# A second projection pass in another order of its products, and x pairs in the value blocks' places

## The chip, the cores and the metric

The kernel runs on one core of a Trainium2 chip. The metric is the device time of one execution in microseconds (us). The kernel before takes 901.85 us, the median of three runs (900.83 to 902.15).

## What is computed

One decoder layer over 512 tokens of width 2048, in float32: a norm, one input projection, two groups of eight attention heads, gates, an output projection, a norm and the residual. `w_in` holds side by side the latents of the MLA heads (768 of the queries, 512 of the keys and values), a rotary key of 64, the MLA gate (1024), queries, keys and values of the FoX heads (1024 each), eight forget logits and the FoX gate (1024).

```python
h = _rms_norm(x, g_pre)
proj = h @ w_in
(q_lat, kv_lat, k_rope_raw, gate_mla,
 fq, fk, fv, f_logit, gate_fox) = jnp.split(proj, split_points, axis=-1)
o_mla = _mla_branch(q_lat, kv_lat, k_rope_raw, g_q, w_uq, g_kv, w_ukv, cos, sin) * jax.nn.silu(gate_mla)
o_fox = _fox_branch(fq, fk, fv, f_logit, b_forget) * jax.nn.silu(gate_fox)
o = jnp.concatenate([o_mla, o_fox], axis=-1) @ w_out
return x + _rms_norm(o, g_post)
```

In the MLA branch both latents are normed, and the queries are `q_lat @ w_uq`, the keys and values `kv_lat @ w_ukv`. In the FoX branch the scores get the running sums of the log forget gates added.

## The kernel before

**Numbers.** TensorE (PE) multiplies halves of a float32 number: each operand is divided into a rounded part `hi` and a rest `lo`, and a product is three matmuls, `hi*hi`, `hi*lo` and `lo*hi`, which stand on lines 152, 153 and 154. Weights come in chunks of 512 KB. `load` or `fill` (lines 236 to 243) brings a chunk into a buffer `raw` by DMA; `divide` (line 283) then makes `whi` on ScalarE (ACT, line 290) and `wlo` on VectorE (DVE, line 291).

**Seven products.** Two large projections are computed with seven block products in place of eight (a Strassen scheme): products `p1`, `p2`, `g5`, `g3`, `g7`, `q6`, `p4`, in which the weights are blocks B11, B12, B21, B22 or sums of them, and the x operand is a block of `h` or a difference of blocks. Sums of weights are made by the DMA itself: a chunk is loaded by SyncE's queue (SP, line 241), and a second block is added into the same buffer by a DMA of GpSimd's (POOL, line 243). A chain, `follow`, says which later chunk takes over a buffer: once a chunk is divided, `fill` of the next one is issued into the same buffer. In the order of before, `g5` begins the chain with B12 in the first pass, and with B11 and an added B12 in the second; `g3` loads B22 afresh, and `g7`, `q6` and `p4` each add one block to what is there.

**Passes.** The first pass, "vg", makes the FoX values (v) and the FoX gate (g), about 65 to 200 us; its `p1` and `p2` accumulate in banks `va` and `ga`. Then come the FoX heads, to about 440 us. The second pass, "lm", makes the MLA latents (l) and the MLA gate (m), with banks `la`, `ma`, then `lg`, `mg`, `lc`, `mc`, `lp`, `mp`, up to 590 us. The MLA heads follow (`mq` and `mk` are queries and keys of a pair of heads, `uA` and so on their values, `sm` scores), and the output projection from about 750 us.

**x operands.** `x_steps(j)` (line 1108) makes, for each of four groups j of the contraction, a pair `xr` of float32 x blocks from `hi` and `lo` (line 1116), and hands it to `away_steps` (line 996), whose `make` computes the four differences `rmg` (line 1015), divides the first into `smg`, and sends each two of them to DRAM (`awaymg`, by POOL, line 1005). `fetch` (line 1044) brings them back as `bmg` or `bmq` when a product needs them, and `part_fetched` divides them (lines 141 and 142, on ACT and DVE). The pairs and the differences lie in the common places `slot` (28 of them).

**Order.** Each engine works through its own queue in order. Which instruction stands where is set by a scheduler from the order of the code; steps put into `todo` are drawn between matmuls, and lists given to `one(..., side=...)` go between the chunks of one product. The forget gate's steps are `forget_sums`, `fs[:3]` and `fs[3:]`: among the latter the transposes `rf` (line 839), its copy (line 840) and the running sum `fz` (line 846). `fox_q` (line 1125) gives the first queries, `fq`, scaled to `fqr` on DVE (line 1130).

**Latents.** `latent(i)` squares a latent block and adds it up in `ls`; `stats_steps` turn a sum (`lbk` of the keys, `lbq` of the queries, by matmuls on PE, line 1471) into a factor, `latent_row(1)` spreads the keys' factor over the partitions (`lrk`, by matmuls), and `latent_part(i)` makes the divided operands `ln`. `mla_k` and the values use `ln6` to `ln9`, the queries `ln0` to `ln5`; `raw153` to `raw155` are the first three chunks of `w_uq`.

Of the kernel before, what the change touches and what calls it, by code (L numbers as in the profile page):

```python
# [19 lines left out]
P = 128  # L20
# [45 lines left out]
def tile_hybrid_layer(  # L66
# [350 lines left out]
    B11, B12, B21, B22 = ((h, c) for h in range(2) for c in range(2))  # L417
    REST = ("g3", B22, None), ("g7", None, B12), ("q6", None, B11), ("p4", None, B21)

    def add_fox(p, n):  # L420
# [6 lines left out]
    for g in "vg":  # L427
        up_chunks.update(prods["p2", g])
    for step in (("g5", None, B12), *REST):
        add_chain("vg", *step)  # L430
# [7 lines left out]
    for j in range(1, 4):  # L438
        chain["m", j] = prods["p2", "m"][j]
    for step in (("g5", B11, B12), *REST):  # L440
        add_chain("lm", *step)
    mla = [{} for _ in range(4)]
    for n in ("q0", "p1", "k0", "q6", "p2", "p4", "g7", "q1", "g5", "k1", "g3", "q2", "k2", "q3", "k3"):
        if (n, "u") in SEVEN:
            add_products([(n, "u")], plain_up)
            if n not in ("p1", "p4"):
                up_chunks.update(prods[n, "u"])
            continue
        p = int(n[1])
        if n[0] == "q":  # L450
            mla[p]["q"] = [
                i
                for k in (4, 0, 2)
                for i in add_chunks(
                    w_uq,
                    [
                        (0, 2 * QK * p, NOPE),
                        (NOPE, 2 * QK * p + QK, NOPE),
                        (2 * NOPE, 2 * QK * p + NOPE, ROPE),
                        (2 * NOPE + ROPE, 2 * QK * p + QK + NOPE, ROPE),  # L460
                    ],
                    2, 2, 2 * QK, k,
                )
            ]
            if p == 0:
                up_chunks.update(mla[p]["q"])
        else:
            mla[p]["k"] = add_chunks(
                w_ukv, [(0, 512 * p, NOPE), (NOPE, 512 * p + NOPE + DV, NOPE)], KVR // P, 4, 2 * NOPE
            )  # L470
# [637 lines left out]
    def x_steps(j):  # L1108

        pair = []  # L1110

        def whole(h, i):
            if not pair:
                pair.extend(slot(f"xr{n}{j}") for n in range(2))
            k = 2 * j + 8 * h + i
            dve.tensor_tensor(out=pair[h][:, i, :], in0=hh[k].bitcast(F32), in1=hl[k].bitcast(F32), op=ALU.add)
            if h and i:
                todo.extendleft(reversed(away_steps("m", j, pair, keep="g5")))

        return [lambda h=h, i=i: whole(h, i) for h in range(2) for i in range(2)]  # L1120
# [149 lines left out]
    wait(1)  # L1270
    todo.extend([*fs[3:], *x_steps(0), *x_steps(1)])
    places = [(g, j) for g in "vg" for j in range(4)]
# [54 lines left out]

    def products(gs, between, out=lambda g, c, half: None):

        G, C, B = {}, {}, {}  # L1330
        for name in ("g5", "g3", "g7", "q6", "p4"):
            for g in gs:
                bank_of = G if name in ("g5", "g3") else B if name == "p4" else C
                if name in ("g5", "p4"):
                    bank_of[g] = banks(name, g, g == gs[1])
                elif name == "g7":
                    C[g] = two_of(proj_bank, f"{g}c")
                rate, side = between.get((name, g), (1, ()))
                one(name, g, bank_of[g], name in ("g5", "g7", "p4"), rate, side)
                if name == "g5":  # L1340
                    place(g, 1, 1)
                    put(g, 1, 1, G[g], ALU.subtract, P1)
                elif name == "g3":
                    place(g, 1, 0)
                    put(g, 1, 0, G[g], ALU.subtract, P1)
                elif name == "g7":
                    put(g, 1, 0, C[g], "less")
                elif name == "q6":
                    put(g, 1, 0, C[g], ALU.add)
                    out(g, 1, 0)  # L1350
                    put(g, 1, 1, C[g], ALU.add)
                    out(g, 1, 1)
                    put(g, 0, 1, C[g], "less")
                else:
                    put(g, 0, 1, B[g], ALU.add)
                    out(g, 0, 1)
                between.get((name, g, "after"), lambda: None)()
# [11 lines left out]
    for g in "vg":  # L1369
# [4 lines left out]
    products(  # L1374
        "vg",
        {
# [58 lines left out]

    LAT = (("q", (4, 5, 0, 1, 2, 3), QR), ("k", (8, 9, 6, 7), KVR))
    raws_of = [None] * 5
# [3 lines left out]
    def raw(i):  # L1441
        return raws_of[(i // 2 + 1) % 5][:, i % 2, :]
# [77 lines left out]
    drain()  # L1520
    for i in (*prods["g5", "l"], prods["g5", "m"][0]):
        fill(i, slot(f"rawl{i}", shape=(P, 1024)))
# [10 lines left out]
    beside.append(room.enter_context(tc.tile_pool(name="rw", bufs=8, reuse_waits="tile")))  # L1533
    for f in f5:
        f()
# [3 lines left out]
    for i in range(2):  # L1539
        for t in range(NT):  # L1540
            pe.transpose(lb[i][:, t * P : (t + 1) * P], l4[:, t, i * P : (i + 1) * P], ident)
        latent(8 + i, lb[i])
    one("p2", "m", A["m"], False, side=[lambda: None, *d5[:2], lambda: (d5[2](), d5[3]())])
    place("m", 0, 0)
# [8 lines left out]

    def later_latents():
        todo.extend(lambda i=i: latent(i, raw(i)) for i in range(4, 8))
        todo.extend([*s1, lambda: latent_part(4), lambda: latent_part(5)])

    def first_latents():
        todo.extend(lambda i=i: latent_part(i) for i in range(4))
        todo.append(lambda: latent_row(1))  # L1560
        todo.extend(lambda i=i: latent_part(i) for i in range(6, 10))

    products(
        "lm",
        {
            ("g5", "l"): (1, f3), ("g5", "m"): (1, d3), ("g3", "l"): (1, f7), ("g3", "m"): (1, d7),
            ("g7", "l"): (1, f6), ("g7", "m"): (1, d6), ("q6", "m", "after"): later_latents,
            ("p4", "l", "after"): first_latents, ("p4", "m"): (2, ()),
        },
# [5 lines left out]
    room.close()  # L1575
    todo.extend(lambda i=i: latent(i, raw(i)) for i in range(4))
    todo.append(lambda: latent_stats(0))
# [7 lines left out]
    qnh, qnl = zip(*(latents[i] for i in LAT[0][1]))  # L1585
    knh, knl = zip(*(latents[i] for i in range(6, 10)))

# [5 lines left out]
    def halves(a):  # L1593
        return [a[:, t, :] for t in range(2)]

    todo.extend(operand_steps("u", 0, (raws_of[4], raws_of[0]), ("sums",), tmp, part_slot))

    def latent_x(half, tokens):
        def parts(kk, t):
            ts = slice((tokens + t) * P, (tokens + t + 1) * P)  # L1600
            return knh[2 * half + kk][:, ts], knl[2 * half + kk][:, ts]

        return parts
# [29 lines left out]
    def mla_k(p, wholes):  # L1633

        kb = [proj_bank(f"mk{p}{i}") for i in range(2)]
        proj_T(mla[p]["k"], [(kb[i], P, two[i]) for i in range(2)], knh, knl, 2, 6)
        kw = [[whole_block(wholes, 2 + i, kb[i]), krw] for i in range(2)]
# [284 lines left out]
```

## Time and profile before

| | |
|---|---|
| median of three runs | 901.85 us |
| the profiled execution's own time | 899.95 us |
| its span | 898.2 us |
| granted clock of TensorE, mean | 0.994 |
| POOL's DMA queue, share of 16 engines | 34.7% |
| SP's DMA queue, share of 16 engines | 48.1% |
| the DMA busy over the whole span, mean | 221 GB/s |

The page gives busy times of each engine, the span in 40 slices, the DMA queues, the chain of work that ended last, and groups of instructions by line. The trace behind it gives the same for any stretch, the waits of an engine with what ended them, and timelines. A busy time above 95% says that an engine leaves little to gain but its waits. The granted clock is the share of full speed at which TensorE ran. A DMA share of 1 says that all 16 engines are busy. Rows with "x3" hold three equal instructions.

### The profile page before, as it was taken

To read this page: it belongs to the slowest core of one execution; us is meant where nothing else is said; L and a number is where in the kernel's file an instruction comes from. 1 tells how busy PE (TensorE), PEld (TensorE's weight loads), DVE (VectorE), ACT (ScalarE), POOL (GpSimd) and SP (SyncE) were. 2 spreads that over 40 slices of the span, in tenths; PEclk is the share of its full clock that TensorE was granted. 3 is DMA by queue.
4 is the path that set the end of the run, shared out by engine and by line. 5 is a ranking of instruction groups with operands and counts; after the bars stand their busy time and mean duration, and the time that the engine had idled before them with its cause. 6 is when DMAs were issued, how large, how long until landed. Compare 5 with 4: busy or idle time off the path is not lost.

```text
span 898.2 us, 13763 instructions
## 1 busy us (share of the span) xinstructions
PE 877.7 (98%) x5078; PEld 773.3 (86%) x5078; DVE 624.6 (70%) x1055; ACT 499.1 (56%) x914; POOL 125.2 (14%) x132
## 2 busy tenths in 40 slices
PE   9999899999999999999989999999999999999996
PEld 8978799999888888889989999987888888887885
DVE  4597756667364744647556767899787886998786
ACT  6934454435245453545634545557676887646383
POOL 1023104451110100000211444000000000000021
PEclk9999999999999999999999999999999999999999
DMA  9499979998588788884799999566959546799878
GB/s 294 128 288 283 277 213 193 222 235 224 110 204 227 192 226 203 230 231 115 253 281 330 280 225 206 116 203 148 222 133 251 149 141 196 230 321 320 263 223 250
DMA packets 128488, 198.41 MB, mean 221 GB/s; under 512 B 16338, under 2 KB 61292, under 8 KB 127396
## 3 DMA queue, kind: packets, MB, share of 16 engines
q1 hardware_dynamic: 101428, 136.28, 48.1%
q0 software_dynamic: 26256, 61.02, 34.7%
q8 instruction: 40, 0.66, 0.3%
q10 hardware_dynamic: 736, 0.22, 0.1%
q14 instruction: 28, 0.23, 0.1%
HBM read 182.60 MB, written 44.25 MB: 253 GB/s over the span
## 4 chain that ended last, share of the span: by engine, by line
PE 79%; DMA 9%; DVE 6%; ACT 3%; issue 2%; POOL 1%; SPq 0%; DVEq 0%; POOLq 0%; ACTq 0%
DMA raw<-in_w_in_dram 5%; PE fk L152 3%; PE fk L154 3%; PE fk L153 3%; PE in L654 3%; PE fq L152 3%; PE fq L153 3%; PE sm L697 3%; PE fq L154 3%; DVE wlo L291 2%; PE mq L152 2%; PE mq L153 2%; PE mq L154 2%; PE sf L697 2%; PE oa L154 2%
## 5 line engine op out<-in xcount | busy, mean ns | idle before, releaser
L291 DVE TENSOR_TENSOR wlo<-raw,whi 128x1024 fp32r<-128x1024 f32 (+3 forms) x159 | 186.9, 1177 | 114.4 <-ACT whi L290 110.9
L290 ACT CAST whi<-raw 128x1024 fp32r<-128x1024 f32 (+3 forms) x159 | 160.5, 1011 | 151.6 <-PE fk L153 35.4
L152 PE MATMUL fk<-h,whi 128*128 128x512 f32 x128 | 52.5, 410 | 0.0
L152 PE MATMUL fq<-h,whi 128*128 128x512 f32 x128 | 50.9, 398 | 0.0
L154 PE MATMUL fk<-h,wlo 128*128 128x512 f32 x128 | 50.3, 393 | 0.0
L154 PE MATMUL fq<-h,wlo 128*128 128x512 f32 x128 | 50.1, 392 | 0.0
L153 PE MATMUL fk<-h,whi 128*128 128x512 f32 x128 | 50.1, 391 | 0.0
L153 PE MATMUL fq<-h,whi 128*128 128x512 f32 x128 | 50.0, 390 | 0.0
L290 ACT CAST whi<-rawv 128x1024 fp32r<-128x1024 f32 x24 | 25.2, 1049 | 42.9 <-PE gg L153 11.0
L291 DVE TENSOR_TENSOR wlo<-rawv,whi 128x1024 fp32r<-128x1024 f32 x24 | 29.3, 1225 | 22.9 <-ACT whi L290 21.3
L290 ACT CAST whi<-rawl 128x1024 fp32r<-128x1024 f32 x25 | 26.2, 1047 | 29.7 <-PE mc L153 7.6
L291 DVE TENSOR_TENSOR wlo<-rawl,whi 128x1024 fp32r<-128x1024 f32 x25 | 30.4, 1224 | 16.8 <-ACT whi L290 16.8
L290 ACT CAST whi<-rawg 128x1024 fp32r<-128x1024 f32 x24 | 25.2, 1052 | 29.6 <-PE vc L154 8.5
L291 DVE TENSOR_TENSOR wlo<-rawg,whi 128x1024 fp32r<-128x1024 f32 x24 | 29.3, 1224 | 13.5 <-ACT whi L290 13.5
L715 ACT ACTIVATE pf<-pf,stf 128x128 f32<-128x128 f32 (+3 forms) x32 | 18.0, 562 | 30.7 <-DVE stf L706 30.7
L243 POOL DMA_DIRECT2D rawl<-in_w_in_dram x20 | 23.9, 1198 | 52.5 <-PE ptf L724 30.9
L1742 POOL DMA_DIRECT2D c<-in_x_dram x8 | 7.0, 1011 | 171.4 <-ACT c L1741 171.4
L654 PE MATMUL in<-whi,h 128*128 128x328 f32 x128 | 30.0, 322 | 0.1
L152 PE MATMUL mq<-ln,whi 128*128 128x512 f32 x72 | 29.1, 404 | 0.0
L154 PEld LDWEIGHTS fk<-h,wlo 128*128 128x128 f32 x128 | 24.0, 188 | 5.3
L154 PEld LDWEIGHTS fq<-h,wlo 128*128 128x128 f32 x128 | 24.0, 188 | 5.3
L154 PE MATMUL mq<-ln,wlo 128*128 128x512 f32 x72 | 28.4, 394 | 0.0
(625 smaller groups left out, 2926.7 us busy)
## 6 DMA issues: line engine op xcount, KB each, us to landing
raw<-in_w_in_dram SPq DMA_DIRECT2D x62, 512.0 KB
raw<-in_w_out_dram SPq DMA_DIRECT2D x32, 512.0 KB
rawl<-in_w_in_dram POOLq DMA_DIRECT2D x20, 512.0 KB, 13.1
rawv<-in_w_in_dram POOLq DMA_DIRECT2D x16, 512.0 KB, 8.3
rawg<-in_w_in_dram POOLq DMA_DIRECT2D x16, 512.0 KB, 11.7
raw<-in_w_in_dram POOLq DMA_DIRECT2D x12, 512.0 KB, 11.2
bmg<-awaymg SPq DMA_DIRECT2D x20, 256.0 KB
rawl<-in_w_in_dram SPq DMA_DIRECT2D x10, 512.0 KB
```

The source lines that it names most:

```text
L152: pe.matmul(o, ah, bh, start=first, stop=False, **kw)
L153: pe.matmul(o, ah, bl, start=False, stop=False, **kw)
L154: pe.matmul(o, al, bh, start=False, stop=last, **kw)
L243: pool.dma_start(to, second, accum_op=ALU.add)
L290: act.copy(hi[:, :m], raw[:, :m])
L291: dve.tensor_tensor(out=lo[:, :m], in0=raw[:, :m], in1=hi[:, :m].bitcast(F32), op=ALU.subtract)
L654: pe.matmul(banks[t][:, :n], a[k][:, tss[t]], b[:, j, :], start=k == 0 and m == 0, stop=k == NK - 1 and m == 2,)
L697: pe.matmul(s[:, :nn], a[:, qs], c[:, :nn], start=(i == 0), stop=(i == len(pairs) - 1))
L715: act.activation(p, p, AF.Exp, bias=st[:, 0:1], scale=unit, accum_out=st[:, 1:2])
L1742: pool.dma_start(to, x[piece(t, c)], accum_op=ALU.add)
```

## The change

There are two parts.

The first concerns the x pairs. They are taken from `v_block`, the four blocks in the pool of the value tiles, and no longer from `slot`; and `x_steps(0)` goes into `todo` ahead of `fs[3:]`.

The second is the order in the second pass: `g3`, `g7`, `q6`, `p4`, `g5` for `g5`, `g3`, `g7`, `q6`, `p4`. `g3`'s chunks begin a chain with one load of B22, and `g5`'s end it with a load of B11 and an added B12. `products` is written so that both orders can be had: which result goes into which block of the output, and which banks are fresh, follow from the order. The operands of `g3` are the first to be fetched, those of `g5` are fetched and divided beside `q6`. With that, the latents come out in another order: 0 to 3 after `p4`, 4 to 9 after `g5`; the query latents are taken as 0 to 5 and `w_uq`'s chunks in the order 0, 2, 4; `latent_row(1)`, `latent_part(6)` to `(9)` and `latent(4)`, `latent(5)` stand behind the pass.

```diff
     REST = ("g3", B22, None), ("g7", None, B12), ("q6", None, B11), ("p4", None, B21)
+    FIRST, LAST_ONE = ("g5", None, B12), ("g5", B11, B12)
...
         chain["m", j] = prods["p2", "m"][j]
-    for step in (("g5", B11, B12), *REST):
+    for step in (*REST, LAST_ONE):
         add_chain("lm", *step)
...
                 i
-                for k in (4, 0, 2)
+                for k in (0, 2, 4)
                 for i in add_chunks(
...
             if not pair:
-                pair.extend(slot(f"xr{n}{j}") for n in range(2))
+                pair.extend(v_block(f"xr{n}{j}") for n in range(2))
             k = 2 * j + 8 * h + i
...
     wait(1)
-    todo.extend([*fs[3:], *x_steps(0), *x_steps(1)])
+    todo.extend([*x_steps(0), *fs[3:], *x_steps(1)])
     places = [(g, j) for g in "vg" for j in range(4)]
...
-    def products(gs, between, out=lambda g, c, half: None):
-
-        G, C, B = {}, {}, {}
-        for name in ("g5", "g3", "g7", "q6", "p4"):
+    def products(gs, names, between, out=lambda g, c, half: None):
+
+        o = {}
+        early = names[0] == "g5"
+        for name in names:
             for g in gs:
-                bank_of = G if name in ("g5", "g3") else B if name == "p4" else C
-                if name in ("g5", "p4"):
-                    bank_of[g] = banks(name, g, g == gs[1])
+                key = {"g3": "g5" if early else "g3", "q6": "g7"}.get(name, name), g
+                fresh = key not in o
+                if fresh:
+                    o[key] = two_of(proj_bank, f"{g}c") if name == "g7" else banks(name, g, g == gs[1])
+                a = o[key]
+                rate, side = between.get((name, g), (1, ()))
+                one(name, g, a, fresh, rate, side)
+                if name == "g3":
+                    place(g, 1, 0)
+                    put(g, 1, 0, a, ALU.subtract, P1)
                 elif name == "g7":
-                    C[g] = two_of(proj_bank, f"{g}c")
-                rate, side = between.get((name, g), (1, ()))
-                one(name, g, bank_of[g], name in ("g5", "g7", "p4"), rate, side)
-                if name == "g5":
+                    put(g, 1, 0, a, "less")
+                elif name == "p4":
+                    put(g, 0, 1, a, ALU.add)
+                    out(g, 0, 1)
+                elif name == "q6":
+                    put(g, 1, 0, a, ALU.add)
+                    out(g, 1, 0)
+                    if early:
+                        put(g, 1, 1, a, ALU.add)
+                        out(g, 1, 1)
+                    else:
+                        place(g, 1, 1)
+                        put(g, 1, 1, a, ALU.subtract, P1)
+                    put(g, 0, 1, a, "less")
+                elif early:
                     place(g, 1, 1)
-                    put(g, 1, 1, G[g], ALU.subtract, P1)
-                elif name == "g3":
-                    place(g, 1, 0)
-                    put(g, 1, 0, G[g], ALU.subtract, P1)
-                elif name == "g7":
-                    put(g, 1, 0, C[g], "less")
-                elif name == "q6":
-                    put(g, 1, 0, C[g], ALU.add)
-                    out(g, 1, 0)
-                    put(g, 1, 1, C[g], ALU.add)
-                    out(g, 1, 1)
-                    put(g, 0, 1, C[g], "less")
+                    put(g, 1, 1, a, ALU.subtract, P1)
                 else:
-                    put(g, 0, 1, B[g], ALU.add)
-                    out(g, 0, 1)
+                    put(g, 1, 0, a, ALU.add)
+                    put(g, 1, 1, a, ALU.add)
                 between.get((name, g, "after"), lambda: None)()
...
-    LAT = (("q", (4, 5, 0, 1, 2, 3), QR), ("k", (8, 9, 6, 7), KVR))
+    LAT = (("q", (0, 1, 2, 3, 4, 5), QR), ("k", (8, 9, 6, 7), KVR))
     raws_of = [None] * 5
...
     drain()
-    for i in (*prods["g5", "l"], prods["g5", "m"][0]):
+    for i in (*prods["g3", "l"], prods["g3", "m"][0]):
         fill(i, slot(f"rawl{i}", shape=(P, 1024)))
...
     beside.append(room.enter_context(tc.tile_pool(name="rw", bufs=8, reuse_waits="tile")))
-    for f in f5:
+    for f in f3:
         f()
...
         latent(8 + i, lb[i])
-    one("p2", "m", A["m"], False, side=[lambda: None, *d5[:2], lambda: (d5[2](), d5[3]())])
+    one("p2", "m", A["m"], False, side=[lambda: None, *d3[:2], lambda: (d3[2](), d3[3]())])
     place("m", 0, 0)
...
-    def later_latents():
-        todo.extend(lambda i=i: latent(i, raw(i)) for i in range(4, 8))
-        todo.extend([*s1, lambda: latent_part(4), lambda: latent_part(5)])
-
     def first_latents():
         todo.extend(lambda i=i: latent_part(i) for i in range(4))
-        todo.append(lambda: latent_row(1))
-        todo.extend(lambda i=i: latent_part(i) for i in range(6, 10))
+        todo.extend(lambda i=i: latent(i, raw(i)) for i in range(4))
+
+    def later_latents():
+        todo.extend(lambda i=i: latent_part(i) for i in (4, 5))
+        todo.extend(lambda i=i: latent(i, raw(i)) for i in (6, 7))
+        todo.extend(s1)
     products(
-        "lm",
+        "lm", ("g3", "g7", "q6", "p4", "g5"),
         {
-            ("g5", "l"): (1, f3), ("g5", "m"): (1, d3), ("g3", "l"): (1, f7), ("g3", "m"): (1, d7),
-            ("g7", "l"): (1, f6), ("g7", "m"): (1, d6), ("q6", "m", "after"): later_latents,
-            ("p4", "l", "after"): first_latents, ("p4", "m"): (2, ()),
+            ("g3", "l"): (1, f7), ("g3", "m"): (1, d7), ("g7", "l"): (1, f6), ("g7", "m"): (1, d6),
+            ("q6", "l"): (1, f5), ("q6", "m"): (1, d5),
+            ("p4", "l", "after"): first_latents, ("g5", "l", "after"): later_latents,
         },
...
     room.close()
-    todo.extend(lambda i=i: latent(i, raw(i)) for i in range(4))
+    todo.append(lambda: latent_row(1))
+    todo.extend(lambda i=i: latent_part(i) for i in range(6, 10))
+    todo.extend(lambda i=i: latent(i, raw(i)) for i in (4, 5))
     todo.append(lambda: latent_stats(0))
...
+    k_parts = []
+    todo.append(lambda: k_parts.extend(zip(*(latents[i] for i in range(6, 10)))))
     todo.extend(operand_steps("u", 0, (raws_of[4], raws_of[0]), ("sums",), tmp, part_slot))
...
             ts = slice((tokens + t) * P, (tokens + t + 1) * P)
-            return knh[2 * half + kk][:, ts], knl[2 * half + kk][:, ts]
+            return [a[2 * half + kk][:, ts] for a in k_parts]
```

What the order of instructions shows, in three places of the program. The number at a name's end tells the instance; `wlo21` is the `wlo` of weight chunk 21.

**DVE in the first pass.** Chunks 19 and 20 are the last two of `ga`'s first product, 21 is the first of `p2`; `rmg53`, `smg53` and `rmg33` are the differences of the last pair, `xr03` and `xr13`. Before:

```order
L291 TENSOR_TENSOR wlo19_973<-rawg2_850,whi19_972 128x1024
L1116 TENSOR_TENSOR xr13_990<-h15_578 128x512
L889 TENSOR_SCALAR angles_1733<-angles_1733 128x128
L291 TENSOR_TENSOR wlo20_1008<-rawg3_852,whi20_1007 128x1024
L1015 TENSOR_TENSOR rmg53_1056<-xr03_989,xr13_990 128x512
L890 TENSOR_SCALAR angles_1733<-angles_1733 128x128
L1015 TENSOR_TENSOR rmg53_1056<-xr03_989,rmg53_1056 128x512
L897 SCALAR_TENSOR_TENSOR angles_1733<-angles_1733 128x128
L1015 TENSOR_TENSOR rmg33_1094<-xr13_990,rmg53_1056 128x512
L291 TENSOR_TENSOR wlo21_1041<-raw21_970,whi21_1040 128x1024
L142 TENSOR_TENSOR smg53_1058<-rmg53_1056,smg53_1058 128x512
```

After, the same place:

```order
L291 TENSOR_TENSOR wlo19_973<-rawg2_849,whi19_972 128x1024
L1117 TENSOR_TENSOR xr03_989<-h6_320 128x512
L1117 TENSOR_TENSOR xr03_989<-h7_353 128x512
L291 TENSOR_TENSOR wlo20_1008<-rawg3_851,whi20_1007 128x1024
L1117 TENSOR_TENSOR xr13_990<-h14_546 128x512
L1117 TENSOR_TENSOR xr13_990<-h15_578 128x512
L291 TENSOR_TENSOR wlo21_1041<-raw21_970,whi21_1040 128x1024
L1016 TENSOR_TENSOR rmg53_1056<-xr03_989,xr13_990 128x512
L291 TENSOR_TENSOR wlo22_1079<-raw22_1005,whi22_1078 128x1024
L142 TENSOR_TENSOR smg53_1058<-rmg53_1056,smg53_1058 128x512
L1016 TENSOR_TENSOR rmg53_1056<-xr03_989,rmg53_1056 128x512
```

`wlo21` stood behind three of the last pair's four differences and now stands ahead of all of them; the rotary `angles` are gone from between. Further ahead in the same queue, where the first queries end (`fqr`), stands after the change:

```order
L1131 SCALAR_TENSOR_TENSOR fqr0_844<-fq00_676,rrow_166 128x512
L1131 SCALAR_TENSOR_TENSOR fqr0_844<-fq01_677,rrow_166 128x512
L841 COPY rf_169<-rf_838 72x512
L1117 TENSOR_TENSOR xr01_857<-h2_232 128x512
L847 SCALAR_TENSOR_TENSOR fz_853<-rf_169,fz_853 8x512
L1117 TENSOR_TENSOR xr01_857<-h3_260 128x512
L1117 TENSOR_TENSOR xr11_858<-h10_434 128x512
L1117 TENSOR_TENSOR xr11_858<-h11_466 128x512
L291 TENSOR_TENSOR wlo15_881<-rawv2_670,whi15_880 128x1024
```

`wlo15` is the third chunk of the first product of v. Before, `rf`, the four `xr` of this pair and `fz` stood ahead of `fqr`; now they stand behind it and ahead of `wlo15`.

**POOL at the start of the second pass.** `rawl113` to `rawl117` and `raw110`, `raw111` are buffers of weight chunks; `awayoa` and `awayog` are writes of the FoX output's operands. Before:

```order
L1005 DMA awayoa111_4739<-gc1_1112 256x1x256
L243 DMA rawl113_4313<-in_w_in_dram 128x2x512
L243 DMA rawl114_4316<-in_w_in_dram 128x2x512
L243 DMA rawl115_4319<-in_w_in_dram 128x2x512
L243 DMA rawl116_4322<-in_w_in_dram 128x2x512
L243 DMA rawl117_4325<-in_w_in_dram 128x2x512
L1005 DMA awayoa110_4885<-gc0_1111 256x1x256
L243 DMA raw110_4401<-in_w_in_dram 128x2x512
L1005 DMA awayog51_4810<-rog51_4795 128x1024
L1005 DMA awayog31_4846<-rog31_4831 128x1024
L243 DMA raw111_4450<-in_w_in_dram 128x2x512
```

After:

```order
L1006 DMA awayoa111_4731<-gc1_1112 256x1x256
L1006 DMA awayoa110_4877<-gc0_1111 256x1x256
L1006 DMA awayog51_4802<-rog51_4787 128x1024
L1006 DMA awayog31_4838<-rog31_4823 128x1024
L243 DMA rawl113_4313<-in_w_in_dram 128x2x512
L243 DMA rawl114_4315<-in_w_in_dram 128x2x512
L243 DMA rawl115_4317<-in_w_in_dram 128x2x512
L243 DMA rawl116_4319<-in_w_in_dram 128x2x512
L243 DMA rawl117_4321<-in_w_in_dram 128x2x512
L243 DMA raw110_4396<-in_w_in_dram 128x2x512
L243 DMA raw111_4445<-in_w_in_dram 128x2x512
```

The seven added loads of before belong to `g5` and are gone here; the writes have moved up. Those of after belong to `g7`.

**SP and PE at the end of the second pass.** SP before, with the last plain load of the pass, the fetches for `g7` and the first `w_uq` chunk, `raw153`:

```order
L241 DMA raw112_4501<-in_w_in_dram 128x2x512
L1044 DMA bmg71_5060<-awaymg31_874 128x512
L1044 DMA bmg72_5091<-awaymg32_965 128x512
L1044 DMA bmg73_5122<-awaymg33_1109 128x512
L268 DMA raw153_5906<-in_w_uq_dram 128x2x128 x2
```

SP after, with the last fetch for `g5`, its loads and the first `w_uq` chunk:

```order
L1045 DMA bmg53_5370<-awaymg53_1074 128x512
L241 DMA rawl113_4313<-in_w_in_dram 128x2x512
L241 DMA rawl114_4315<-in_w_in_dram 128x2x512
L241 DMA rawl115_4317<-in_w_in_dram 128x2x512
L241 DMA rawl116_4319<-in_w_in_dram 128x2x512
L241 DMA rawl117_4321<-in_w_in_dram 128x2x512
L241 DMA raw110_4396<-in_w_in_dram 128x2x512
L241 DMA raw111_4445<-in_w_in_dram 128x2x512
L268 DMA raw153_5896<-in_w_uq_dram 128x2x128 x2
```

The loads of `g5` now stand at the pass's end, and the `w_uq` chunk behind seven of them. PE in the third chunk of `w_uq`, before (`lbq` is the sum of the query latents):

```order
L154 MATMUL mq01_6081<-ln2_5972,wlo155_6092 128x512
L152 MATMUL mq02_6082<-ln2_5972,whi155_6091 128x512
L153 MATMUL mq02_6082<-ln2_5972,whi155_6091 128x512
L1471 MATMUL lbq_6143<-ones_101,ls_4560 128x1 x4
L154 MATMUL mq02_6082<-ln2_5972,wlo155_6092 128x512
L152 MATMUL mq00_6080<-ln3_5975,whi155_6091 128x512
```

and after:

```order
L154 MATMUL mq00_6074<-ln5_5932,wlo155_6086 128x512
L152 MATMUL mq01_6075<-ln5_5932,whi155_6085 128x512
L153 MATMUL mq01_6075<-ln5_5932,whi155_6085 128x512
L1480 MATMUL lbq_6160<-ones_101,ls_4554 128x1 x4
L154 MATMUL mq01_6075<-ln5_5932,wlo155_6086 128x512
L152 MATMUL mq02_6076<-ln5_5932,whi155_6085 128x512
```

`lbq` stood beside `ln2`, the chunk's first latent, in the last group of its first half; now it stands beside `ln5`, its second. `lrk`, before in the middle of the last product's gate chunks, now stands between the matmuls of the first `w_uq` chunk.

7 lines of the change are left out of this document (3 added, 4 removed).

## The prediction

> **What bounds the kernel now.** I read the page first: the busy table, then the waits of the matmul engine, then stretches around its largest waits.
>
> ```profile
> PE 877.7 (98%) x5078; PEld 773.3 (86%) x5078; DVE 624.6 (70%) x1055; ACT 499.1 (56%) x914; POOL 125.2 (14%) x132
> ```
>
> ```profile
> PE va L153 <- DVE wlo L291: 5.2, 1, 5.2
> ...
> PE lg L152 <- ACT whi L290: 1.7, 1, 1.7
> ...
> PE lg L154 <- DVE wlo L291: 0.8, 1, 0.8
> PE rf L839 <- DVE rft L806: 0.7, 1, 0.7
> PE sm L697 <- DVE rq L142: 0.7, 1, 0.7
> ...
> PE mg L154 <- DVE wlo L291: 0.4, 1, 0.4
> ...
> PE mk L152 <- ACT mw L126: 0.3, 1, 0.3
> ```
>
> PE is busy for 98% of the span, and the change removes no matmul: it can only win PE's waits and the clock lost behind them, or add some. The waits list gives each as total, times and longest (us). `va` is the first pass, `lg` and `mg` are the first sum product of the second pass, `sm` and `mk` the start of the MLA heads. Now the stretches that hold them (busy us of PE, PEld, DVE, ACT, POOL; granted clock; DMA share; GB/s):
>
> ```profile
> 88.00:93.50 5.50, 0.34 (x2) 0.14 (x1) 2.01 (x3) 1.24 (x2) 0.00 (x0) 0.95 1.11 255
> 93.50:97.00 3.50, 3.50 (x10) 2.80 (x11) 3.36 (x9) 0.77 (x2) 0.56 (x1) 0.59 1.06 259
> ...
> 469.00:476.00 7.00, 4.59 (x25) 4.21 (x24) 5.67 (x7) 6.09 (x9) 0.95 (x2) 0.76 1.08 324
> ...
> 500.00:570.00 70.00, 70.00 (x586) 70.00 (x585) 49.81 (x59) 33.41 (x39) 26.22 (x22) 1.00 1.10 215
> 570.00:590.00 20.00, 20.00 (x168) 19.92 (x167) 16.91 (x32) 14.79 (x25) 0.00 (x0) 1.00 0.52 148
> ```
>
> Each big wait also costs clock: 5.50 x 0.05 + 3.50 x 0.41 = 1.7 us at 88 to 97, and 7.00 x 0.24 = 1.7 us at 469 to 476. From 500 to 570 PE never waits although the DMA engines are full; from 570 they are half empty. So there is room late in the second pass for transfers that now crowd its start.
>
> **Part 1, the x pairs.** Why `va` waits is in the chain of waits and in DVE's timeline:
>
> ```profile
> 77.66 13.73 DMA awaymg<-rmg
> ```
>
> ```profile
> 91.49 0.69 DVE L1015 TENSOR_TENSOR rmg<-xr,rmg 128x512 f32<-128x512 f32 x1 [7.88 <-DMA awaymg<-rmg]
> 92.09 1.22 DVE L291 TENSOR_TENSOR wlo<-raw,whi 128x1024 fp32r<-128x1024 f32 x1
> ```
>
> An `rmg` sum waits 7.88 us until an earlier pair's sums have left for DRAM (13.73 us), because it writes into the same slot. Behind it on DVE stands the `wlo` that PE wants. In the new order this first plain `wlo` stands ahead of the last pair's sums, and the pairs no longer take `slot` places. So the 5.2 us go, with their 1.7 us of clock. The 0.7 us of `rf` go as well, since its transposes now stand behind the last `fq` matmul: 5.2 + 1.7 + 0.7 = 7.6 us.
>
> What is late next? The work that ran beside `fq` now falls behind it, ahead of the third and fourth `wlo` of the first product:
>
> ```profile
> 59.57 0.68 DVE L840 COPY rf<-rf 72x512 f32<-72x512 f32 x1
> 60.17 0.68 DVE L1015 TENSOR_TENSOR rmg<-xr,xr 128x512 f32<-128x512 f32 x1
> 60.87 1.22 DVE L846 TENSOR_TENSOR_SCAN fz<-rf,fz 8x512 f32<-8x512 f32 x1
> 62.12 1.23 DVE L291 TENSOR_TENSOR wlo<-rawv,whi 128x1024 fp32r<-128x1024 f32 x1
> ...
> 65.67 1.28 DVE L1130 SCALAR_TENSOR_TENSOR fqr<-fq,rrow 128x512 f32<-128x512 f32 x2
> 66.87 1.22 DVE L291 TENSOR_TENSOR wlo<-rawv,whi 128x1024 fp32r<-128x1024 f32 x1
> 68.00 1.90 DVE L1116 TENSOR_TENSOR xr<-h 128x512 f32<-128x512 f32 x3
> 69.80 1.23 DVE L291 TENSOR_TENSOR wlo<-rawv,whi 128x1024 fp32r<-128x1024 f32 x1
> ```
>
> And PE's timeline, where `va` starts and where its third and fourth chunks want their `wlo`:
>
> ```profile
> 65.42 0.39 PE L152 MATMUL va<-whi,h 128*128 128x512 f32 x1
> 65.65 0.39 PE L153 MATMUL va<-wlo,h 128*128 128x512 f32 x1
> ...
> 71.09 0.39 PE L153 MATMUL va<-wlo,h 128*128 128x512 f32 x1
> ...
> 73.81 0.39 PE L153 MATMUL va<-wlo,h 128*128 128x512 f32 x1
> ```
>
> Start to start, a 128x512 row of DVE takes 0.60 us, the scan 1.25, `fqr` x2 1.20, a `wlo` 1.14 (1.23 to its result); a `va` matmul takes 0.23. With `rf`'s wait gone `va` starts 0.7 us sooner, at 64.7; four transposes (0.4) stand before it, so `fq` ends at 64.3. From there DVE has `fqr` 1.20, `rf` 0.60, one `xr` 0.60, the scan 1.25, three `xr` 1.80 and the third `wlo` 1.23: ready at 71.0, while PE wants it at 71.09 - 0.7 = 70.4. That is **0.6 us** of wait. For the fourth, DVE has seven 0.60 rows and a `wlo`: 1.14 + 4.20 + 1.23 from the third's start, 5.3 us after its result; PE has 73.81 - 71.09 = 2.7 us of matmuls and five more that the new order pulls ahead (one of 0.23, four 256-column ones of half that): 3.4. That is **1.9 us**. The next ones come within 0.1 us of their need. New waits: 2.6 us, bounded by 0 (the scheduler's pulled matmuls suffice) and 4 (both sums a half too small).
>
> Does the clock halve behind 1.9 us? `rf`'s 0.7 us did not show in the clock; 1.7 + 0.8 us within three microseconds did. 1.9 is nearer to the second, so I add **1.7**, with 0 and 1.7 as ends. Part 1: -7.6 + 2.6 + 1.7 = -3.3 us.
>
> The Trainium skill, "TensorE: Matmul & The Clock Gate", Part 1, has another rule: the clock goes to half "after ≥1 idle window (~3.4µs)". By that a 1.9 us wait costs no clock, and the time would be that of the first rival below. The row 469:476 speaks against it: 0.76 with 2.4 us of idle time in two pieces.
>
> **Part 2, the start of the second pass.** ACT's timeline where `lg` waits:
>
> ```profile
> 469.21 0.62 ACT L141 CAST bmg<-bmg 128x512 fp32r<-128x512 f32 x1 [5.04 <-DMA bmg<-awaymg]
> 469.73 1.04 ACT L290 CAST whi<-rawl 128x1024 fp32r<-128x1024 f32 x1
> ```
>
> Of the DMA issues from 440 to 500 (KB each, median us to landing), of the chain of waits, and of stretches:
>
> ```profile
> rawl<-in_w_in_dram POOLq DMA_DIRECT2D x7, 512.0 KB, 13.4
> ```
>
> ```profile
> 457.37 9.68 DMA raw<-in_w_in_dram
> ```
>
> ```profile
> 490.00:500.00 10.00, 9.59 (x80) 9.38 (x79) 7.46 (x10) 5.58 (x8) 3.58 (x4) 1.00 1.05 389
> ...
> 530.00:540.00 10.00, 10.00 (x86) 10.00 (x85) 7.59 (x9) 4.70 (x6) 3.58 (x3) 1.00 1.13 206
> ```
>
> ACT waits 5.04 us for `bmg`, an operand fetched while the engines carry plain loads, fetches and POOL's adds; the `whi` that PE wants stands behind. A 512 KB add at 206 GB/s takes 0.524 / 0.206 = 2.55 us of all engines, a plain load at 389 GB/s 1.35. With `g3` first, five adds (12.8 us of transfer) are gone from 443 to 469, and three more from the 23 us after. `bmg`, fetched from 457.8, then has over 10 us for some 4 us of transfers ahead of it. So 1.7 + 0.8 + 0.4 us of waits and 1.7 us of clock go: **-4.6 us**; bounds 0 (another transfer keeps `bmg` late) and -4.6. On POOL the writes `awayoa` and `awayog` now stand ahead of the first adds, not behind them; the adds behind are wanted a product later, so the wait hides.
>
> **Part 3, the end of the second pass.** `g5` now needs, in each chunk, a load by SP after the chunk before it in the buffer is cast, then POOL's add behind that load. POOL's timeline, and the DMA issues from 500 to 560:
>
> ```profile
> 537.14 1.20 POOL L243 DMA_DIRECT2D raw<-in_w_in_dram  x1 [1.69 <-DVE wlo L291]
> ...
> 554.42 1.20 POOL L243 DMA_DIRECT2D raw<-in_w_in_dram  x1 [1.69 <-DVE wlo L291]
> ```
>
> ```profile
> rawl<-in_w_in_dram POOLq DMA_DIRECT2D x13, 512.0 KB, 13.1
> ```
>
> Chunks pass at (554.42 - 537.14) / 6 = 2.88 us, a product of eight in 23.0. Less the two casts (1.05 and 1.23), 20.7 us are there from one cast to the landing needed for the next. The last add of `p4` goes out one step before, so it lands 13.1 - 2.9 = 10.2 us in, and the first `g5` add 2.55 later: 12.8, so 7.9 in hand. From there 1.35 + 2.55 = 3.9 us of transfer meet each 2.88, which eats 7 x 1.02 = 7.1: the eighth is 0.8 us ahead. On SP the first `w_uq` load now stands behind seven of these loads and beside the last adds; it is wanted only after the eighth chunk, but its transfer uses those 0.8 us up, so I take **+0.5 us**, with 0 and the third rival's 12.4 as ends.
>
> At the MLA start `lbq`, the sums of the query latents, stands six matmuls later in the third `w_uq` chunk, and the two `lrk` matmuls stand inside the first: 8 x 0.23 = 1.8 us later for the chain that ends in `mk`, which already waits 0.3. Half of it is hidden by the `uA` products: **+0.9 us**, bounds 0 and 2.6 (all of it, and `sm` later by 0.8).
>
> **Sum.** -3.3 - 4.6 + 0.5 + 0.9 = -6.5 us. The profiled execution took 899.95 us (span 898.2); that gives 893.45. It is 1.9 us below the median of the runs, 901.85, and I put the same difference on the median: **895.4 us**.
>
> **The rivals.**
> - *The clock does not halve behind the new wait*: -8.2, 893.7 us. For it: one piece of idle time, not two; against it: the 0.76 row. Chance 0.2.
> - *The new waits do not come at all and the tail is covered*: -7.6 - 4.6 = -12.2, 889.7 us. For it: DVE's row sums are within 2 us of PE's. Chance 0.1.
> - *Slower: the crowd only moves to the end.* If a load before `g5` takes the 9.68 us of 457.37 and its add the 13.4 of that stretch, the chain is 9.7 + 1.2 + 13.4 = 24.3 against 20.7: PE waits 3.6 us at the first chunk and 7.1 more over the rest, and 1.7 of clock: 12.4. In place of the 0.5 that is +5.4, 907.3 us. It decides from a chain above 20.7 us, and turns the sign where the last chunk is 7 us late. For it: engines at 1.13 until 560; against it: from 570 they are half empty. Chance 0.14.
> - *It does not do what it says*: `bmg` is late for the plain loads' sake and the second pass keeps its 4.6 us: -1.9, 900.0 us. For it: loads and fetches stay where they were; against it: five adds are twelve of the 29 us before. Chance 0.14.
>
> **How the numbers follow.** The forecast has 0.42: 895.4, itself from 893 to 898 by the bounds of the waits. The range is 889.5 to 902.5: it takes in all but the slower rival and leaves out about 0.15. A measurement can tell about 0.2% (1.8 us) from no change. Faster by more: 0.42 + 0.2 + 0.1 and half of the last rival, rounded down for partial stalls, 0.77; within it: 0.11; slower: 0.12.
>
> **What would show it.** Right: no `rmg` wait of several us on DVE, `va` waiting under 3 us near 70 to 77 in place of 5.2 at 88; no `lg` wait at 469 and a clock of 1.00 there; DMA share well below 1 somewhere in 450 to 470, and above 1 until about 580. Wrong: `wlo` of `g5` late at the pass's end with POOL's adds landing over 13 us after issue, `mk` or `sm` waiting over 3 us, or the clock at 0.5 in a new place.

## The result and the profile after

The changed kernel takes **906.31 us**, the median of five runs (905.76 to 908.89); the kernel before takes 901.16 (900.61 to 902.15, five runs). The ratio is 1.0061, with a 95% interval of 1.0044 to 1.0078. It is slower by some 0.6%, where 895.4 us and a gain of 0.7% were forecast. The profiled execution took 905.88 us with a span of 904.0 and a mean granted clock of 0.991; that is 5.9 us over the profiled execution of before.

The waits of PE after (in all, times, longest, in us) answer to the list shown of before:

```profile
PE lbk L1480 <- DVE ls L1462: 6.6, 1, 6.6
PE va L153 <- DVE wlo L291: 2.8, 1, 2.8
...
PE mk L152 <- ACT mw L126: 1.6, 1, 1.6
PE uC L152 <- ACT suq L141: 1.3, 1, 1.3
...
PE ga L154 <- DVE wlo L291: 1.2, 2, 0.8
...
PE ga L152 <- ACT whi L290: 0.3, 1, 0.3
```

`lg`, `mg`, `rf` and `sm` are gone from the list, as meant. A wait that was not there before now leads it: `lbk`, the sum of the key latents, 6.6 us. The same stretches of after (busy us of PE, PEld, DVE, ACT, POOL; granted clock; DMA share; GB/s):

```profile
70.00:75.00 5.00, 2.19 (x10) 1.51 (x9) 4.97 (x8) 1.67 (x2) 1.17 (x1) 0.99 0.61 195
75.00:80.00 5.00, 4.96 (x18) 3.81 (x17) 5.00 (x8) 1.05 (x1) 1.73 (x4) 0.67 1.08 269
...
469.00:476.00 7.00, 7.00 (x60) 7.00 (x60) 3.23 (x5) 3.62 (x4) 3.34 (x3) 1.00 1.12 256
570.00:580.00 10.00, 9.97 (x84) 9.76 (x82) 6.24 (x9) 4.38 (x6) 1.19 (x1) 1.00 0.92 214
580.00:590.00 10.00, 3.46 (x16) 3.49 (x17) 4.53 (x11) 3.27 (x4) 0.00 (x0) 0.68 1.01 279
590.00:600.00 10.00, 10.00 (x51) 8.87 (x50) 6.30 (x15) 4.25 (x10) 0.00 (x0) 0.81 0.00 0
```

The row 469:476 is PE busy throughout at full clock, where it was idle for 2.4 of 7 us and at 0.76 before. The rows from 580 on hold what that gain was paid with: PE busy for 3.46 of 10 us, and the clock low until about 594 (10.00 x 0.19 = 1.9 us lost at half speed are 3.8 us of the last row).

Waits, and clock lost while PE is busy (in us of full speed), by stage:

| stage | before | after | measured | forecast |
|---|---|---|---|---|
| first pass: `va`, `rf`, `ga`, clock at 75 to 97 | 7.6 | 6.0 | -1.6 | -3.3 |
| second pass, start: `lg`, `mg`, clock at 469 to 476 | 4.6 | 0 | -4.6 | -4.6 |
| second pass, end: `lbk`, clock at 580 to 600 | 0 | 10.2 | +10.2 | +0.5 |
| MLA start: `sm`, `mk`, `uA`, `uC` | 2.0 | 2.9 | +0.9 | +0.9 |
| sum | | | +4.9 | -6.5 |

The 6.0 are 2.8 of `va`, 1.5 of `ga` and 4.96 x 0.33 = 1.6 of clock. The 10.2 are 6.6 of `lbk`, 10.00 x 0.19 = 1.9 of clock in the last row and 1.7 in the row before it: the wait ends at 586.5, and from then to 590 PE ran at half speed (3.46 x 0.5). The 4.9 stand against 5.9 between the two executions. The rest is not in the waits: PE's busy time went from 877.7 to 880.8 us, 3.1 more, of which the clock in the table explains 1.8. What makes the other 1.3 was not followed.

**Where the 6.6 us come from.** The chain of waits, start and length:

```profile
556.70 18.63 DMA raw<-in_w_in_dram
575.40 0.49 issue
575.89 6.78 DMA raw<-in_w_in_dram
582.76 1.05 ACT whi L290
583.84 1.23 DVE wlo L291
585.07 0.61 DVE ls L1462
585.70 0.70 DVE ls L1462
586.40 0.14 issue
586.54 1.84 PE lbk L1480 x8
```

The first row is SP's load of B11 into `raw112`, the last chunk of `g5`; the third is POOL's add of B12 into it. The load was issued at 556.70 and took 18.63 us. Only then could the add go, 6.78 us, then the two casts. And what PE waits for is not the chunk: it is two sums of squares `ls` of latents, which on DVE stand behind the chunk's `wlo`. The queues of SP and POOL (start, us, queue, line, operation; in brackets the idle time ahead and what ended it):

```profile
549.10 3.25 SPq L241 DMA_DIRECT2D raw<-in_w_in_dram  x2
552.45 4.14 SPq L268 DMA_DIRECT2D raw<-in_w_uq_dram  x4
556.70 3.71 SPq L241 DMA_DIRECT2D raw<-in_w_in_dram  x1
```

```profile
543.64 1.18 POOL L243 DMA_DIRECT2D rawl<-in_w_in_dram  x1 [9.60 <-DMA rawl<-in_w_in_dram]
...
553.04 1.19 POOL L243 DMA_DIRECT2D rawl<-in_w_in_dram  x1 [4.75 <-DVE ln L145]
557.00 1.18 POOL L243 DMA_DIRECT2D rawl<-in_w_in_dram  x1 [2.78 <-DMA rawl<-in_w_in_dram]
561.05 1.19 POOL L243 DMA_DIRECT2D raw<-in_w_in_dram  x1 [2.87 <-DVE wlo L291]
565.02 1.18 POOL L243 DMA_DIRECT2D raw<-in_w_in_dram  x1 [2.78 <-DMA raw<-in_w_in_dram]
575.89 1.19 POOL L243 DMA_DIRECT2D raw<-in_w_in_dram  x1 [9.69 <-DMA raw<-in_w_in_dram]
```

Four DMAs of `w_uq` stand ahead of the last `g5` load on SP: seven of the eight loads go ahead of them and the eighth behind. Together the four hold 384 KB, less than one chunk. POOL's fourth to seventh adds go out 3.99 us apart ((565.02 - 553.04) / 3); the eighth comes 10.87 us after the seventh. ACT's casts of the fourth to the eighth chunk each end an idle time that the add's landing ends; the fourth is

```profile
564.77 1.05 ACT L290 CAST whi<-rawl 128x1024 fp32r<-128x1024 f32 x1 [2.55 <-DMA rawl<-in_w_in_dram]
```

Its add was issued at 553.04, 11.7 us before. PE, though, still had time in hand. The `wlo` of the fourth and of the seventh chunk on DVE, and the first matmuls of PE that read them:

```profile
565.85 1.23 DVE L291 TENSOR_TENSOR wlo<-rawl,whi 128x1024 fp32r<-128x1024 f32 x1 [2.37 <-ACT whi L290]
...
576.15 1.21 DVE L291 TENSOR_TENSOR wlo<-raw,whi 128x1024 fp32r<-128x1024 f32 x1
```

```profile
569.97 0.28 PE L154 MATMUL lg<-bmg,wlo 128*128 128x256 f32 x1
...
578.61 0.28 PE L154 MATMUL mg<-bmg,wlo 128*128 128x256 f32 x1
```

The fourth `wlo` is ready at 567.1, 2.9 us before its first matmul, the seventh at 577.4, 1.2 us before. At 2.88 us a chunk PE would have read the eighth at 581.5; it is ready at 585.1. So the chain loses slowly over seven chunks, and by 3.6 us against PE's need at the eighth.

### The profile page after: what moved, and what is told of

It reads as the page before. It is cut to its first block, busy times and chain, and to the rows that moved or that the text cites. A ratio compares the mean times of both kernels' runs of the same rounds, so it can differ in the third digit from the quotient of the medians.

```text
span 904.0 us, 13768 instructions
## 1 busy us (share of the span) xinstructions
PE 880.8 (97%) x5078; PEld 776.2 (86%) x5078; DVE 627.9 (69%) x1059; ACT 500.0 (55%) x914; POOL 124.9 (14%) x132
## 4 chain that ended last, share of the span: by engine, by line
PE 81%; DMA 8%; DVE 5%; ACT 2%; issue 2%; SPq 0%; POOL 0%; DVEq 0%; ACTq 0%; POOLq 0%
DMA raw<-in_w_in_dram 3%; PE fk L152 3%; PE fk L154 3%; PE fk L153 3%; PE fq L152 2%; PE fq L154 2%; PE sm L698 2%; PE fq L153 2%; PE in L655 2%; PE mq L152 2%; PE mq L153 2%; PE mq L154 2%; PE sf L698 2%; PE oa L154 2%; PE oa L152 2%
```

## The experiments

The theory: the second pass's new order wins its start as forecast and loses more at its end, because the last `g5` chunk is late (load behind `w_uq`, then the add) and `lbk` stands behind it. The x part on its own gains a little. The rivals: the loss is in the transfers as such, or in the place of `lbk`, or in the x part. "Before" is the kernel before, timed on the same chip; its medians there were 900.97 to 901.16.

**The x part alone**, on the kernel before:

```diff
-                pair.extend(slot(f"xr{n}{j}") for n in range(2))
+                pair.extend(v_block(f"xr{n}{j}") for n in range(2))
...
-    todo.extend([*fs[3:], *x_steps(0), *x_steps(1)])
+    todo.extend([*x_steps(0), *fs[3:], *x_steps(1)])
```

> The kernel before with the first part alone (x pairs in the value blocks' places, their steps ahead of the forget sums). Theory (the time is the sum of PE's waits and of the clock lost behind them): the first pass does what it does in the changed kernel, where it lost 5.2 + 0.7 us of waits and 1.5 of clock and got 2.8 + 0.4 + 0.3 + 0.8 us of new waits and 1.7 of clock, so -1.4 us: about 899.8 us beside 901.2. The lg wait of 1.7 us at the second pass stays. Rival (the first part is the loss): over 903 us.

Measured: 898.84 us (897.01 to 899.75), ratio 0.997 [0.9958, 0.9982]. `va` waits 2.8 us, `lg` and `mg` wait as before, nothing waits at the end of the second pass. This half of the change gains, by 1 us more than expected beforehand and by 1.1 us less than the 3.3 of the forecast.

**The second part alone**, the changed kernel with the x pairs and their steps as before:

```diff
-                pair.extend(v_block(f"xr{n}{j}") for n in range(2))
+                pair.extend(slot(f"xr{n}{j}") for n in range(2))
...
-    todo.extend([*x_steps(0), *fs[3:], *x_steps(1)])
+    todo.extend([*fs[3:], *x_steps(0), *x_steps(1)])
```

> The kernel before with the second part alone (order of the products in the second pass, with all that belongs to it). Theory (the loss is the last product's late chunk): the lg waits go (-4.1 us), lbk waits 6 to 7 us near 580 with 3 to 4 us of clock behind it, the start of the MLA heads costs about 1 more: +7, about 908 us. Rival (both parts only lose together, through a shift of phase): within 2 us of 901.2.

Measured: 907.35 us (907.1 to 907.96), ratio 1.0071 [1.0056, 1.0086]. PE's waits there:

```profile
PE lbk L1480 <- DVE ls L1462: 7.8, 1, 7.8
PE va L153 <- DVE wlo L291: 4.8, 1, 4.8
```

The loss is this part's. The two halves alone differ from before by -2.2 and +6.3 us; the change as a whole by +5.2.

**The pairs' place without the order of their steps**, the first of the two diff lines of the x part alone, on the kernel before:

> The kernel before with the pairs in the value blocks' places and nothing else; the forget sums stay ahead. Theory (the 7.88 us of DVE came from the shared places, and the new va wait of 2.8 us comes from the order of steps): no rmg wait, no va wait over 1 us, rf waits its 0.7 as before: -5.2 - 1.5 = about 894.5 us. Rival (with the pairs out of the shared places the wait only moves to another instruction there): a wait of 2 us or more between 70 and 100 us, 898 or more.

Measured: 897.28 us (897.25 to 897.92), ratio 0.9959 [0.9945, 0.9973]. It gains, but less than expected: a new wait of 1.6 us stands where the theory had none.

```profile
PE va L153 <- DVE wlo L291: 1.8, 2, 1.6
...
PE rf L839 <- DVE rft L806: 1.2, 1, 1.2
```

```profile
75.00:80.00 5.00, 3.38 (x17) 2.58 (x15) 5.00 (x8) 1.45 (x2) 1.80 (x2) 1.00 1.02 292
```

The clock stays at 1.00 behind it, where the 2.8 us of the changed kernel brought 0.67. Its median is 1.6 us below that of the whole x part: moving `x_steps(0)` ahead of `fs[3:]` gains nothing by these medians, though the intervals of the two ratios overlap.

**Without the last product's add.** B12 is left out of `g5`'s weights in the second pass, so that its chunks are one plain load each:

```diff
-    FIRST, LAST_ONE = ("g5", None, B12), ("g5", B11, B12)
+    FIRST, LAST_ONE = ("g5", None, B12), ("g5", B11, None)
```

> The changed kernel without the addition of B12 in the last product: its chunks hold B11 alone, so the product has other weights than it should. Theory (the add behind the load makes the last chunk late): lbk waits under 1 us, the clock stays at 1.00 from 570 to 600, so 906.3 - 6.6 - 3.6 = about 896 us. Rival (lbk waits since the sums it needs stand behind the last wlo on DVE and the latents come late in this order, whatever the transfers do): over 3 us of lbk wait stay, 902 us or more.

Measured: 895.22 us (894.7 to 895.79), ratio 0.9936 [0.9921, 0.9951], 11.1 us below the changed kernel. The stretch that was at 3.46 and 0.68:

```profile
580.00:590.00 10.00, 10.00 (x60) 8.65 (x59) 8.33 (x21) 5.52 (x12) 0.00 (x0) 1.00 0.46 154
```

`lbk` is not in its list; `mk` at 1.6 and `uC` at 1.3 stay. Without the adds nothing of the stage's 10.2 us is left, though the last load still stands behind the four `w_uq` DMAs and `lbk` keeps its place. Neither costs anything here. With the adds 4 MB of transfers are gone too, so this run does not tell the chain of load and add from the bytes.

**The first MLA queries' `w_uq` loads behind the last `g5` load on SP**, with all the rest as in the changed kernel:

```diff
-                nc.sync.dma_start(to, first)
+                state["fill"] = nc.sync.dma_start(to, first).ins
...
-            last = (nc.sync if cnt >= P or small is None else small).dma_start(
...
+            with tc.issue_after(state["fill"]) if i in mla[0].get("q", ()) else nullcontext():
+                last = (nc.sync if cnt >= P or small is None else small).dma_start(
```

> The changed kernel, with the w_uq loads of the first MLA queries held behind the last load of the last product on SP's queue; nothing else. Theory (that load took 18.6 us since the four pieces of the first w_uq chunk were ahead of it in the queue): it lands 5 to 7 us sooner, lbk waits under 2 us in place of 6.6, the clock is lost for at most one stretch of 3.4 us: 898 to 901 us beside 906.3. Rival (the DMA engines are full from 540 on and the order of the pieces doesn't matter): lbk waits 4 us or more, over 903 us.

Measured: 899.57 us (897.73 to 900.65), ratio 0.9981 [0.9971, 0.999], 6.7 us below the changed kernel. The last add on POOL, PE's wait and the stretch:

```profile
568.49 1.19 POOL L243 DMA_DIRECT2D raw<-in_w_in_dram  x1 [2.78 <-DMA raw<-in_w_in_dram]
```

```profile
PE lbk L1481 <- DVE ls L1463: 2.8, 1, 2.8
```

```profile
580.00:590.00 10.00, 8.36 (x46) 8.35 (x47) 5.36 (x15) 2.20 (x4) 0.00 (x0) 0.66 0.73 225
```

With nothing but the queue order changed, the add goes out 7.4 us sooner, again four us behind the seventh, and the wait falls from 6.6 to 2.8 us. So 3.8 us of it, and a part of the clock, belong to the `w_uq` loads. The time is as expected; the wait was to be under 2 us. Where the other 2.8 us come from, the next two runs show.

**`lbk` behind the product**: the key latents' sums are taken out of the list between the matmuls and run after the pass.

```diff
         todo.extend(lambda i=i: latent(i, raw(i)) for i in (6, 7))
-        todo.extend(s1)
...
     drain()
+    for s in s1:
+        s()
```

> The changed kernel, with the sums of the key latents (lbk) behind the last product and not in its third gate chunk; the w_uq loads as in the changed kernel. Theory (part of the wait comes from lbk's place: the ls sums it needs stand behind the last wlo on DVE, and 12 plus 24 matmuls of the product stand behind lbk on PE): PE's wait moves 12 matmuls on, to the last chunk's whi and wlo, and falls from 6.6 us to 3 to 4; clock lost once; about 902 us. Rival (the whole 6.6 us are the late transfer): the same 6 us at another instruction, 905 to 907 us.

Measured: 905.53 us (905.14 to 905.8), ratio 1.005 [1.0035, 1.0065]. PE's waits:

```profile
PE mk L152 <- ACT mw L126: 3.5, 1, 3.5
PE mg L152 <- ACT whi L290: 3.0, 1, 3.0
...
PE mg L154 <- DVE wlo L291: 0.8, 1, 0.8
```

The wait shrinks from 6.6 to 3.8 us: that much the late chunk costs the gate product itself, and the rest was `lbk`'s place ahead of matmuls that could have run. But `mk`, which needs the keys' factor, now waits 3.5 in place of 1.6, and the clock is low behind it (0.67 in 610:620). The time is the rival's, its reason is not: the 6.6 us did not move as one. The median is 0.8 us below the changed kernel's and the intervals of the ratios overlap, so moving `lbk` alone gains nothing that can be told.

**Both edits together:**

> Both edits together on the changed kernel. Theory (a late load and lbk's place add up): no PE wait over 1 us between 560 and 600, clock 1.00 there: -6.6 - 3.6 = about 896 us, as without the last additions (895.2). Rival (full DMA engines): a wait of 2 us or more for the last chunk stays, 899 or more.

Measured: 899.26 us (898.4 to 900.48), ratio 0.9981 [0.9971, 0.999]. Of the gate product's waits one row is left:

```profile
PE mg L154 <- DVE wlo L292: 0.2, 1, 0.2
```

So the 6.6 us are accounted for: 3.8 by the `w_uq` loads, 2.8 by `lbk`'s place. Each edit alone leaves the other's part, and both leave 0.2. The chain of loads and adds by itself hardly holds PE up. But `mk` waits 3.5 us and the clock is low behind it:

```profile
605.00:610.00 5.00, 5.00 (x15) 3.96 (x16) 4.91 (x12) 0.27 (x1) 0.00 (x0) 0.66 1.00 190
```

That is 3.3 us over what was expected, and no faster than the queue order alone. The statistic's cost moves; it does not go. `va` waits 4.0 us in this run, 1.2 more than in the changed kernel.

**Both edits, and the x steps in their old order** (the pairs stay in the value blocks' places):

> The same as both together, and the x steps behind the forget sums as in the kernel before; the pairs stay in the value blocks' places. Theory (waits of the stages add up): the first pass as with the pairs alone, with 3.9 us of waits and no lost clock in place of 4.4 and 1.7, so 2 us under both together: about 894 us, faster than both kernels. Rival (the first pass and the second are coupled, or the clock halves here): no better than both together.

Measured: 897.51 us (896.99 to 898.12), ratio 0.9958 [0.9945, 0.9972]. `va` waits 1.6 us and not 4.0, with the clock at 1.00; `mk` still waits 3.5. It missed its number, 894, by what stays at `mk`.

**The queue order alone, and the x steps in their old order:**

> The changed kernel with the x steps behind the forget sums again (pairs still in the value blocks' places) and the w_uq loads behind the last product's last load. Theory (stages add up): uq_behind took 899.6; the first pass is about 2 us better, so about 897.5 us; lbk waits 2 to 3 us and mk 1.6. Rival (the halved clock falls elsewhere when the first pass shifts): 899 us or more.

Measured: 897.17 us (895.48 to 900.21), ratio 0.9959 [0.9947, 0.997]. `lbk` 2.7 us, `mk` 1.6, `uC` 1.2: as expected.

**The same, with the last key latents and `lbk` ahead of two of the query latents' operands:**

```diff
     def later_latents():
-        todo.extend(lambda i=i: latent_part(i) for i in (4, 5))
         todo.extend(lambda i=i: latent(i, raw(i)) for i in (6, 7))
         todo.extend(s1)
+        todo.extend(lambda i=i: latent_part(i) for i in (4, 5))
```

> The same, and the key latents' squares and sums ahead of latent_part(4) and (5), so that the ls sums stand ahead of the last wlo on DVE and lbk one chunk sooner on PE. Theory (the place of the ls sums on DVE makes the rest of the wait, and the sooner chain shortens mk's): lbk waits under 0.7 us, mk under 1, no lost clock from 570 to 630: 892 to 894 us, under both kernels and under the pairs alone (897.3). Rival (the last chunk's add is late all the same): PE waits 2 us or more at the last gate chunk, 896 us or more.

Measured: 896.21 us (894.07 to 898.56), ratio 0.9949 [0.9934, 0.9965]. Its waits in the profiled execution, which at 894.07 was the fastest of its six runs, and the stretch:

```profile
...
PE va L153 <- DVE wlo L292: 1.6, 1, 1.6
PE lbk L1481 <- DVE ls L1463: 1.5, 1, 1.5
PE mk L152 <- ACT mw L126: 1.3, 1, 1.3
```

```profile
580.00:590.00 10.00, 10.00 (x61) 8.91 (x61) 8.63 (x22) 6.22 (x13) 0.00 (x0) 1.00 0.60 183
```

None of the three is over 2 us, and the clock is at 1.00 where it was 0.68. The expectation was missed all the same: `lbk` was to wait under 0.7 us and `mk` under 1, for 892 to 894 us. The median lies in the rival's range, without the rival's wait at the last gate chunk. This version beats both kernels: 10.1 us under the changed one, 4.8 under before. Its interval overlaps those of the two versions above it and that of the pairs' place alone, so the last edit's own gain is not settled, and neither is whether the new order of the second pass, mended so far, gains anything over the pairs' place alone.

## Why the prediction was wrong

**The start of the second pass** came as forecast, in its size and in its way: -4.6 us. The adds are gone from there, the DMA share in 450:460 is 0.66 where it was 1.10, ACT no longer waits for `bmg`, and the clock is at 1.00 from 469 to 476.

**The MLA start** has the forecast's number, +0.9 us, in part by luck. `mk` went from 0.3 to 1.6, as the later chain says; but `uC` (1.3), which was not foreseen, came in the place of `sm` (1.3) and `uA` (0.4), which went.

**The x pairs** had the right sign and half the size: -1.6 against -3.3. The `rmg` wait went, and the clock fell behind the new wait as chosen. What the sum lacked is `ga`: 1.5 us, not foreseen, whose cause was not followed. That `va` waits 2.8 us where 2.6 were reckoned is luck: the 0.6 at the third chunk became 2.8, and the 1.9 at the fourth, with the clock at 0.67 by then, became nothing. The working took DVE to be free for `fqr` at 64.3. In the changed kernel the rotary `angles` stand ahead of it:

```profile
62.26 0.23 DVE L883 CAST angles<-angles 128x128 f32<-128x128 int32 x1 [5.61 <-DMA angles<-in_positions_dram]
...
66.74 1.28 DVE L1131 SCALAR_TENSOR_TENSOR fqr<-fq,rrow 128x512 f32<-128x512 f32 x2
...
72.31 1.22 DVE L291 TENSOR_TENSOR wlo<-rawv,whi 128x1024 fp32r<-128x1024 f32 x1
```

DVE sat idle 5.61 us until their input had landed and worked on them until `fqr` began, 2.4 us later than reckoned; the third `wlo` was ready at 73.5 and not at 71.0. On whether the clock halves behind 1.9 us by itself, the run with 1.6 us in one piece says no for that length. The rule of the Trainium skill, "TensorE: Matmul & The Clock Gate", Part 1, that the clock halves after an idle window of about 3.4 us, agrees with those 1.6 us and not with the 2.8 us behind which 75:80 shows 0.67; the measurement decides.

**The end of the second pass is the step that failed**: "the eighth is 0.8 us ahead ... so I take +0.5 us" became +10.2. The pace of the chain was not at fault: 3.9 us of load and add to a chunk were reckoned, and the adds went out 3.99 us apart. Its working left 4.8 us in hand at the fourth chunk and 1.8 at the seventh; 2.9 and 1.2 were there. With the two pieces below out of the way the product waited 0.2 us. What failed is what the working said of the eighth chunk and of those behind it.

- *SP's order was read and priced too low.* The text saw that "the first `w_uq` load now stands behind seven of these loads", and let its transfer use up 0.8 us. There are eight chunks: the eighth load stands behind those `w_uq` loads. It took 18.63 us, and its add went out 10.87 us after the seventh in place of four. This is 3.8 of the 6.6 us, shown by moving only those loads.
- *Whoever stands behind the late chunk was not looked for.* The working does not name `lbk`. Its sums stand behind the last `wlo` on DVE, and on PE `lbk` stands ahead of gate matmuls whose chunk was there. This is the other 2.8 us, shown by moving `lbk`, alone and together with the loads.
- *No clock was reckoned for that wait.* The clock fell behind the 6.6 us and cost 3.6 more.

The slower rival, "the crowd only moves to the end", came near in size: 12.4 us against 10.2, 907.3 against 906.31. That is luck for the most part. It was right that the chain of load and add decides, since without the adds the loss is gone; but it put 3.6 us on the first chunk and 7.1 on the others, and PE waited for none of the first seven. What spoke against it, engines half empty from 570 on, was read from the kernel before, where no adds are left by then; the changed kernel's are at 0.92 from 570 to 580 and 1.01 from 580 to 590.

## What to carry to other kernels

Moving transfers out of a crowded stage helps only if the stage that receives them can cover the whole chain of each chunk. A pace that is right for the chain as a whole (3.9 us reckoned, 3.99 measured) says nothing of the one chunk whose load stands elsewhere in the queue. Go to the last link first: look up what stands ahead of it in its own queue, and what stands behind it on each engine, since a small sum queued behind a late operand stops work that has its operands. Where two edits come together, time each alone: here one gained 2.2 us and the other lost 6.3.

## What the runs showed of the hardware

The granted clock. One wait of 1.6 us left it at 1.00 (75:80 with the pairs' place alone). One of 2.8 us brought 0.67 in the five microseconds behind it, and one of 3.5 us 0.66. Behind the 6.6 us of `lbk` the stretches 580:590 and 590:600 are at 0.68 and 0.81: 6.6 us of wait cost 10.2. The length alone did not set the price: `lbk` waited 2.8 us with the queue order alone and 2.7 with the x steps in their old order as well; 580:590 is at 0.66 in the first and 0.83 in the second.

The DMA. The same 512 KB load of `raw112`, issued at 556.70 behind four `w_uq` DMAs, took 18.63 us to land. With these behind it, its add went out four us after the seventh in place of 10.87, though no transfer was left out. Why 384 KB ahead of it cost that much, no run here shows.
